# Order of the splits in an MLP's products, and its last two blocks run as one

## The chip, the cores and the metric

One core of one Trainium2 chip runs the whole kernel. The metric is the device time of one execution in microseconds (us), as the median of several.

## The reference

A trunk of two layers over T = 1040 tokens (16 meta tokens and 1024 of the sequence), model width 1024, all in float32. Each layer has a mixer and an MLP of 4096 hidden features with squared ReLU; a final norm follows.

```python
def rmsnorm(x, w):
    return x * lax.rsqrt(jnp.mean(x * x, -1, keepdims=True) + EPS) * w
def sq_relu_mlp(h, w_up, w_down):
    return jnp.square(jax.nn.relu(h @ w_up)) @ w_down
for layer in range(2):
    hn = rmsnorm(h, norm_mix[layer])
    h = h + (even_mixer(hn, ...) if layer == 0 else ssd_mixer(hn, ...))
    h = h + sq_relu_mlp(rmsnorm(h, norm_mlp[layer]), mlp_w_up[layer], mlp_w_down[layer])
h = rmsnorm(h, norm_final)[:, 16:]
```

## The kernel before

**Precision.** TensorE (PE) multiplies in a shortened float format (`fp32r`). So each factor is split into a rounded part `hi` and the rest `lo`, and each product is three matmuls: hi by hi, hi by lo and lo by hi (`mm3`, L176 to L181). A split is a cast on ScalarE (ACT) and, behind it, a subtraction `x - hi`. In `split2` (L379) these are L385 and L386; the subtraction runs on GpSimd (POOL) for a weight and on VectorE (DVE) for a token factor. `load_w` (L159) does the same for a whole row of 1024 weights that has come by DMA: cast L173, subtraction L174, on DVE in the MLP.

**Tokens.** The residual `h` stays in SBUF, features on the partitions, tokens on the free axis. Token tiles are i = 0, 1, 2 of 400, 384 and 256 tokens (384, 384 and 256 where the meta tokens are left out: layer 1's MLP).

**The MLP** (`mlp`, L389). The 4096 hidden features are 32 rows of 128, taken as 16 blocks of two (f = 0, 1). `up_unit` (L357) computes one token tile of one row: 24 matmuls into a PSUM tile `mm`, then the rectifier times the token's norm factor (DVE, L372) and the square (ACT, L373) into the hidden tiles `sq`. A block has six such units. Each block's share of the down projection is then added to `h`. The two rows of a block and the two halves of the tokens (520 each in layer 0, 512 in layer 1) form 2 x 2 quarters of the hidden values (`b11` to `b22`), and the weights have four quarters likewise (`w11` to `w22`).

- Blocks 0 to 13 take `seven` products (keys 1, 2, 5, 6, 3, 4, 7) of combined quarters in place of eight. POOL forms the combinations in `ca` (weights) and `cb` (tokens); both go through `split2`, into a ring of six buffers `pc`. A product (`product`, L486) is 48 matmuls of 260 columns in layer 0 and 24 of 512 in layer 1; its results are evicted from the PSUM tile `pd` by DVE's addition (L502) into `h` or into one of three running sums `acc1`, `acc6`, `acc7`. In block 0 those sums are written by ACT's copy (L500).
- Block 14 takes the `eight` plain products, two at a time, so four double products (c11, c21, c22, c12). Between them stand the six up units of block 15, and `combine` (L504, additions L505), which joins the three sums to `h`.
- Block 15 is the last part (L562 to L594). Its hidden values are split (L569 on ACT, L570 on DVE) into the room of `acc1` and `acc6`; then, for each token tile, each of the 8 output tiles n takes 6 matmuls and is evicted by L583 on DVE. Behind each eviction stand the next norm's squares (L587) and, in layer 1, the scaling by the final norm's weight (L591).

The next norm goes on from there: `token_sums` (L243) sums over the features on PE (L250), `rsqrt` (L184 to L196) takes the reciprocal root on DVE in three Newton steps, `token_bcast` (L263) spreads it on PE (L267), and `apply` (L287) scales, casts and splits the token tile for mixer 1 (L293, L295, L297). In layer 1 `final` (L321) multiplies by the spread root (L337 on DVE, L335 on POOL) and stores.

PSUM has eight banks. In the MLP's wide stage `pd` has three tiles of two banks, and `ps` (the `mm` tiles) two of one; else `ps` has four. In `mlp` the pieces of a product are split two products ahead of its matmuls:

```python
        sw = lambda x: self.split2(mp, x, pool)
        sx = lambda x: self.split2(mp, x, v)
            yield "1", [(sw(w11), sx(b11))]
```

The order on each engine is that of a list scheduler, which places the instructions when the kernel is built, by the program's order and its estimate of when each can start. Each engine then works in that order, and semaphores keep the dependences.

## Time and profile before

| | |
|---|---|
| median of 3 runs | 2789.8 us (2785.27 to 2791.72) |
| the profiled execution | 2793.77 us, its span 2792.0 us |
| instructions | 44635 |
| PE busy | 2677.5 us (96%), 17121 matmuls |
| PE's weight loads | 2554.3 us (91%) |
| DVE busy | 2118.9 us (76%), 3901 instructions |
| ACT busy | 1104.8 us (40%), 2275 |
| POOL busy | 1077.8 us (39%), 1005 |
| granted clock of PE, mean | 0.982 |

All times are of one profiled execution, from the span's start. Layer 0's MLP takes its first product at about 417 us; its last part runs from 1081.6 to 1110.5 us, and mixer 1 begins there. Layer 1's last part ends at 2773.2 us, and the last norm and the stores fill the rest. A busy share is a mean over stages with different limits. In a timeline's rows, `A<-B` is the tile written and the tiles read, `x2` says that two such instructions in a row are told as one, and brackets hold the idle time just before an instruction and what ended it.

### The profile page before, as it was taken

To read this page: it belongs to the slowest core of one execution; us is meant where nothing else is said; L and a number is where in the kernel's file an instruction comes from. 1 tells how busy PE (TensorE), PEld (TensorE's weight loads), DVE (VectorE), ACT (ScalarE), POOL (GpSimd) and SP (SyncE) were. 2 spreads that over 40 slices of the span, in tenths; PEclk is the share of its full clock that TensorE was granted. 3 is DMA by queue.
4 is the path that set the end of the run, shared out by engine and by line. 5 is a ranking of instruction groups with operands and counts; after the bars stand their busy time and mean duration, and the time that the engine had idled before them with its cause. 6 is when DMAs were issued, how large, how long until landed. Compare 5 with 4: busy or idle time off the path is not lost.

```text
span 2792.0 us, 44635 instructions
## 1 busy us (share of the span) xinstructions
PE 2677.5 (96%) x17121; PEld 2554.3 (91%) x17121; DVE 2118.9 (76%) x3901; ACT 1104.8 (40%) x2275; POOL 1077.8 (39%) x1005
## 2 busy tenths in 40 slices
PE   7998999999999999999999999999989999999997
PEld 7887999999999998899999999999978999999996
DVE  9887466777777787977767767677797777777786
ACT  4555353223322223453434434344454333333333
POOL 3212115445454432242333333334444455455432
PEclk9999999999999999999999999999999999999998
DMA  4432411111111110121212212123312111111101
GB/s 163 114 79 58 140 43 54 43 50 50 46 54 43 54 31 29 45 85 54 72 57 63 75 56 70 58 63 95 102 60 68 53 54 46 54 57 45 51 31 65
DMA packets 117909, 176.35 MB, mean 63 GB/s; under 512 B 13376, under 2 KB 47936, under 8 KB 117568
## 3 DMA queue, kind: packets, MB, share of 16 engines
q1 hardware_dynamic: 117408, 173.34, 20.0%
q8 instruction: 135, 2.21, 0.3%
q14 instruction: 78, 0.64, 0.1%
q10 hardware_dynamic: 288, 0.15, 0.0%
HBM read 158.34 MB, written 8.72 MB: 60 GB/s over the span
## 4 chain that ended last, share of the span: by engine, by line
PE 72%; DVE 19%; ACT 3%; issue 3%; POOL 2%; DMA 2%; SPq 0%; DVEq 0%; ACTq 0%; POOLq 0%
PE mm L179 16%; PE mm L180 16%; PE mm L181 16%; PE pd L179 6%; PE pd L181 6%; PE pd L180 6%; DVE xbc L1261 3%; DVE wlo L174 2%; DVE acc L502 2%; PE mm L1371 1%; ACT whi L173 1%; PE sm L1375 1%; DVE pc L386 1%; PE mm L1368 1%; PE sm L267 1%
## 5 line engine op out<-in xcount | busy, mean ns | idle before, releaser
L179 PE MATMUL mm<-hi,whi 128*128 128x384 f32 (+2 forms) x3120 | 1020.3, 327 | 19.7 <-ACT whi L173 9.8
L180 PE MATMUL mm<-lo,whi 128*128 128x384 f32 (+2 forms) x3120 | 1007.9, 323 | 0.8 <-DVE lo L940 0.4
L181 PE MATMUL mm<-hi,wlo 128*128 128x384 f32 (+2 forms) x3120 | 1005.7, 322 | 2.7 <-POOL wlo L174 2.7
L179 PEld LDWEIGHTS mm<-hi,whi 128*128 128x128 f32 x3120 | 593.8, 190 | 30.6 <-ACT whi L173 11.1
L180 PEld LDWEIGHTS mm<-lo,whi 128*128 128x128 f32 x3120 | 593.0, 190 | 8.8 <-POOL lo L297 2.0
L181 PEld LDWEIGHTS mm<-hi,wlo 128*128 128x128 f32 x3120 | 595.1, 191 | 3.8 <-POOL wlo L174 3.5
L179 PE MATMUL pd<-pc 128*128 128x260 f32 (+1 forms) x1272 | 408.0, 321 | 14.4 <-DVE acc L502 12.0
L180 PE MATMUL pd<-pc 128*128 128x260 f32 (+1 forms) x1272 | 404.2, 318 | 0.0
L181 PE MATMUL pd<-pc 128*128 128x260 f32 (+1 forms) x1272 | 404.1, 318 | 0.0
L502 DVE TENSOR_TENSOR h<-h,pd 128x520 f32<-128x520 f32 (+1 forms) x360 | 312.7, 871 | 68.0 <-PE pd L181 53.4
L386 POOL TENSOR_TENSOR pc<-draw,pc 128x512 fp32r<-128x512 f32 x96 | 131.7, 1375 | 419.9 <-ACT pc L385 409.6
L179 PEld LDWEIGHTS pd<-pc 128*128 128x128 f32 x1272 | 238.8, 188 | 34.9 <-DVE acc L502 18.7
L373 ACT ACTIVATE sq<-s 128x384 f32<-128x384 f32 (+2 forms) x192 | 94.3, 491 | 409.7 <-DVE s L372 409.6
L181 PEld LDWEIGHTS pd<-pc 128*128 128x128 f32 x1272 | 239.3, 188 | 16.6
L180 PEld LDWEIGHTS pd<-pc 128*128 128x128 f32 x1272 | 239.2, 188 | 13.1
L386 POOL TENSOR_TENSOR pc<-ca,pc 128x512 fp32r<-128x512 f32 x112 | 156.0, 1393 | 235.2 <-ACT pc L385 231.9
L173 ACT CAST whi<-wraw 128x512 fp32r<-128x512 f32 x286 | 167.2, 618 | 155.6 <-PE mm L180 137.6
L372 DVE SCALAR_TENSOR_TENSOR s<-mm,rb 128x384 f32<-128x384 f32 (+2 forms) x192 | 98.8, 515 | 170.4 <-PE mm L181 156.3
L1261 DVE SCALAR_TENSOR_TENSOR xbc<-s,cols,xbc 128x400 f32<-128x400 f32 (+2 forms) x288 | 202.7, 704 | 24.1 <-ACT xbc L1259 21.5
L502 DVE TENSOR_TENSOR acc<-acc,pd 128x520 f32<-128x520 f32 (+1 forms) x234 | 189.1, 859 | 4.0 <-PE pd L181 4.0
L174 DVE TENSOR_TENSOR wlo<-wraw,whi 128x512 fp32r<-128x512 f32 x224 | 167.0, 764 | 17.1 <-ACT whi L173 10.3
L386 DVE TENSOR_TENSOR pc<-cb,pc 128x520 fp32r<-128x520 f32 (+1 forms) x112 | 149.3, 1333 | 38.7 <-ACT pc L385 38.7
(381 smaller groups left out, 4424.6 us busy)
## 6 DMA issues: line engine op xcount, KB each, us to landing
wraw<-in_mlp_up SPq DMA_DIRECT2D x128, 256.0 KB
draw<-in_mlp_down SPq DMA_DIRECT2D x120, 256.0 KB
wraw<-in_ssd_in SPq DMA_DIRECT2D x120, 256.0 KB
csb<-csd SPq DMA_DIRECT2D x64, 256.0 KB
sa<-ecd SPq DMA_DIRECT2D x128, 64.0 KB
wraw<-in_ssd_out SPq DMA_DIRECT2D x32, 256.0 KB
wraw<-in_ev_in SPq DMA_DIRECT2D x24, 256.0 KB
wraw<-in_ev_out SPq DMA_DIRECT2D x18, 256.0 KB
```

The source lines that it names most:

```text
L173: nc.scalar.copy(hi[:, s], raw)
L174: e.tensor_tensor(out=lo[:, s], in0=raw, in1=hi[:, s].bitcast(F32), op=ALU.subtract)
L179: nc.tensor.matmul(pt, lhsT=whi, rhs=xhi, start=first, stop=False)
L180: nc.tensor.matmul(pt, lhsT=whi, rhs=xlo, start=False, stop=False)
L181: nc.tensor.matmul(pt, lhsT=wlo, rhs=xhi, start=False, stop=last)
L267: self.nc.tensor.matmul(st[:, o:o + l], lhsT=y[:l, i:i + 1].broadcast_to([l, P]), rhs=self.ident[:l, :l], start=True, stop=True)
L372: nc.vector.scalar_tensor_tensor(out=r, in0=pt[:, :w], scalar=0.0, in1=rbs[i], op0=ALU.max, op1=ALU.mult)
L373: nc.scalar.activation(out=dst[:, o - t0:o - t0 + w].bitcast(F32), in_=r, func=AF.Square)
L386: e.tensor_tensor(out=lo, in0=x, in1=hi.bitcast(F32), op=ALU.subtract)
L502: v.tensor_tensor(out=d, in0=d, in1=src, op=ALU.add)
L1261: v.scalar_tensor_tensor(out=ot, in0=raw[:, k:k + w], scalar=cw(k), in1=ot, op0=ALU.mult, op1=ALU.add)
L1368: nc.tensor.matmul(py[:, j * P:j * P + P], lhsT=H[:, 2 * j:2 * j + 2].rearrange("p r q -> p (r q)"), rhs=r["C"], start=True, stop=True)
```

## The change

- `pair` splits the token factor of a product first and then the weight factor; all seven products of a block use it. Before, the weight came first.
- `eight` is gone. Block 14 takes no products of its own any more. Its two rows and the two of block 15 are the four rows f = 0 to 3 of one plain product: in the last part each output tile takes 12 matmuls, not 6. For the first token tile the rows of block 14 of output tiles 0 to 3 come ahead of those of block 15.
- The three sums are joined to `h` during the six up units of block 15, with no products between. Block 14's hidden values are split in the same place, on ACT and POOL (L548, L549), into the room of `acc1` and `acc6`. Those of block 15 are split on ACT and DVE into the room of `acc7` and one more pair of `sq` tiles.
- The four weight rows are loaded as whole rows: two during the last two products of block 13, one at the fourth up unit, one behind the sixth (into the buffers `draw`). Their raw quarters are not loaded for block 14.
- In `psum`, the pool `ps` is taken before `pd`.

```diff
@@ -121,8 +121,8 @@
         self.pstack = st = ExitStack()
         self.npsum += 1
         pool = lambda name, bufs: st.enter_context(self.tc.tile_pool(name=f"{name}{self.npsum}", bufs=bufs, space=PSUM))
+        self.ps = pool("ps", 2 if wide else 4)
         self.pd = pool("pd", 3) if wide else None
-        self.ps = pool("ps", 2 if wide else 4)
         self.pss = None if wide else pool("pss", 4)
 
     def load_h(self, i, k0=0, k1=KT):
@@ -161,6 +161,8 @@
         pool = pool or self.wp
         if tag == "pc":
             hi, lo = (self.piece(pool)[:, :1024] for _ in range(2))
+        elif tag == "draw":
+            hi, lo = ([pool.tile([P, 512], F32R, name=tag, bufs=6) for _ in range(2)] for _ in range(2))
         else:
             bufs = 2 if tag == "o" else None
             hi = pool.tile([P, 1024], F32R, name=f"{tag}hi", bufs=bufs)
@@ -170,8 +172,9 @@
             s = slice(q * 512, q * 512 + 512)
             raw = self.wp.tile([P, 512], F32, name="wraw", bufs=3)
             nc.sync.dma_start(raw, ap[:, s])
-            nc.scalar.copy(hi[:, s], raw)
-            e.tensor_tensor(out=lo[:, s], in0=raw, in1=hi[:, s].bitcast(F32), op=ALU.subtract)
+            h, l = (hi[q], lo[q]) if tag == "draw" else (hi[:, s], lo[:, s])
+            nc.scalar.copy(h, raw)
+            e.tensor_tensor(out=l, in0=raw, in1=h.bitcast(F32), op=ALU.subtract)
         return hi, lo
 
     def mm3(self, pt, whi, wlo, xhi, xlo, first, last):
@@ -436,8 +439,9 @@
             (b11, b12), (b21, b22) = ((q[:, :hw].bitcast(F32), q[:, hw:].bitcast(F32)) for q in sq[b])
             return raws.pop(b), (b11, b12, b21, b22)
 
-        sw = lambda x: self.split2(mp, x, pool)
-        sx = lambda x: self.split2(mp, x, v)
+        def pair(w, x):
+            x = self.split2(mp, x, v)
+            return [(self.split2(mp, w, pool), x)]
 
         def seven(b):
 
@@ -450,37 +454,23 @@
                 if x0 is not None:
                     pool.tensor_tensor(out=cb, in0=x0, in1=x1, op=ALU.subtract)
 
-            yield "1", [(sw(w11), sx(b11))]
-            yield "2", [(sw(w12), sx(b21))]
+            yield "1", pair(w11, b11)
+            yield "2", pair(w12, b21)
             comb(w21, w22, ALU.add, b12, b11)
-            yield "5", [(sw(ca), sx(cb))]
+            yield "5", pair(ca, cb)
             comb(ca, w11, ALU.subtract, b22, cb)
-            yield "6", [(sw(ca), sx(cb))]
+            yield "6", pair(ca, cb)
             comb(w12, ca, ALU.subtract, None, None)
-            yield "3", [(sw(ca), sx(b22))]
+            yield "3", pair(ca, b22)
 
             pool.tensor_tensor(out=cb, in0=b21, in1=cb, op=ALU.subtract)
-            yield "4", [(sw(w22), sx(cb))]
+            yield "4", pair(w22, cb)
             comb(w11, w21, ALU.subtract, b22, b12)
-            yield "7", [(sw(ca), sx(cb))]
-
-        def eight(b):
-
-            (w11, w12, w21, w22), (b11, b12, b21, b22) = quarters(b)
-            a = sw(w11), sw(w12)
-            x = sx(b11), sx(b21)
-            yield "c11", list(zip(a, x))
-            a = sw(w21), sw(w22)
-            yield "c21", list(zip(a, x))
-            x = sx(b12), sx(b22)
-            yield "c22", list(zip(a, x))
-            a = sw(w11), sw(w12)
-            yield "c12", list(zip(a, x))
+            yield "7", pair(ca, cb)
 
         acc = {k: mp.tile([P, 4, hw], F32, name=f"acc{k}", bufs=1) for k in "167"}
         H = lambda r, c: self.H[:, 4 * r:4 * r + 4, halves[c]]
-        dest = {"1": acc["1"], "6": acc["6"], "7": acc["7"], "2": H(0, 0), "5": H(1, 1), "3": H(0, 1), "4": H(1, 0),
-                "c11": H(0, 0), "c12": H(0, 1), "c21": H(1, 0), "c22": H(1, 1)}
+        dest = {"1": acc["1"], "6": acc["6"], "7": acc["7"], "2": H(0, 0), "5": H(1, 1), "3": H(0, 1), "4": H(1, 0)}
         step = 2 if len(subs) == 1 else 1
 
         def product(key, pairs, copy):
@@ -520,66 +510,92 @@
         for n in range(0, 4, 2):
             d = H(0, 1)[:, n:n + 2]
             v.tensor_tensor(out=d, in0=d, in1=H(1, 1)[:, n:n + 2], op=ALU.subtract)
-        items = (it for b in range(NB - 1) for it in (seven(b) if b < NB - 2 else eight(b)))
+        items = (it for b in range(NB - 2) for it in seven(b))
         queue = deque()
-        fetch = lambda: queue.append(next(items))
+
+        def fetch():
+            it = next(items, None)
+            if it:
+                queue.append(it)
+
         fetch()
         fetch()
+        wd = []
         for b in range(NB - 2):
             u = ups(b + 1)
+            end = b == NB - 3
             for j in range(7):
-                if j == 3:
+                if j == 3 and not end:
                     rows(b + 1)
-                last = b == NB - 3 and j > 4
-                if not last:
-                    fetch()
-                elif j == 6:
-                    fetch()
+                fetch()
                 product(*queue.popleft(), b == 0)
+                if end and j > 4:
+                    wd.append(self.load_w(down[2 * NB - 9 + j], mp, "pc"))
                 next(u, None)
             for _ in u:
                 pass
+
         u = ups(NB - 1)
         com = combine()
-        for j in range(4):
-            if j < 3:
-                fetch()
-            else:
-                wd = [self.load_w(down[2 * NB - 2], mp, "pc")]
-            product(*queue.popleft(), False)
-            for _ in range(2):
-                next(u, None)
+        hid = []
+
+        def room(k):
+            t = mp.tile([P, 4, hw], F32R, name=f"acc{k}", bufs=1)
+            return [t[:, n:n + 2].rearrange("p a b -> p (a b)") for n in (0, 2)]
+
+        def parts(hl, q, c, e):
+            h, l = (z[:, c] for z in hl)
+            nc.scalar.copy(h, q[:, c].bitcast(F32))
+            e.tensor_tensor(out=l, in0=q[:, c].bitcast(F32), in1=h.bitcast(F32), op=ALU.subtract)
+
+        for j in range(6):
+            if j in (2, 4):
+                hid.append(room("16"[j // 2 - 1]))
+                for c in (slice(0, hw), slice(hw, 2 * hw)):
+                    parts(hid[-1], sq[NB - 2][j // 2 - 1], c, pool)
+            next(u, None)
+            if j == 3:
+                wd.append(self.load_w(down[2 * NB - 2], mp, "pc"))
+            next(com, None)
+            if j == 0 or j == 2:
                 next(com, None)
         for _ in u:
             pass
         for _ in com:
             pass
-        wd.append(self.load_w(down[2 * NB - 1], mp, "pc"))
+        wd.append(self.load_w(down[2 * NB - 1], mp, "draw"))
+        hid.append(room("7"))
+        hid.append(hidden(NB))
         self.psum(False)
         if nxt == "nmix1":
             self.ahead_bc()
-
-        hid = []
-        for k in "16":
-            t = mp.tile([P, 4, hw], F32R, name=f"acc{k}", bufs=1)
-            hid.append([t[:, n:n + 2].rearrange("p a b -> p (a b)") for n in (0, 2)])
         for o, w in tls:
-            c = slice(o - t0, o - t0 + w)
-            for (h, l), q in zip(hid, sq[NB - 1]):
-                nc.scalar.copy(h[:, c], q[:, c].bitcast(F32))
-                v.tensor_tensor(out=l[:, c], in0=q[:, c].bitcast(F32), in1=h[:, c].bitcast(F32), op=ALU.subtract)
+            for f in range(2):
+                parts(hid[2 + f], sq[NB - 1][f], slice(o - t0, o - t0 + w), v)
+
+        def last(pt, i, n, f):
+            o, w = tls[i]
+            (ah, al), (xh, xl) = wd[f], (z[:, o - t0:o - t0 + w] for z in hid[f])
+            if f == 3:
+                ah, al = ah[n // 4], al[n // 4]
+            ns = slice(n % 4 * P, n % 4 * P + P) if f == 3 else slice(n * P, n * P + P)
+            self.mm3(pt[:, :w], ah[:, ns], al[:, ns], xh, xl, f == 0, f == 3)
+
         end = nxt == "nfin"
         for i, (o, w) in enumerate(tls):
             off = o - TT[i][0]
             hs = lambda n: self.h[i][:, n, off:off + w]
-            pts = {}
             for n in range(KT):
-                for f, m in ((f, m) for f in range(2) for m in (range(n, n + 4) if n % 4 == 0 else ())):
-                    if f == 0:
-                        pts[m] = self.mm()
-                    ms = slice(m * P, (m + 1) * P)
-                    h, q = (z[:, o - t0:o - t0 + w] for z in hid[f])
-                    self.mm3(pts[m][:, :w], wd[f][0][:, ms], wd[f][1][:, ms], h, q, f == 0, f == 1)
+                if n == 0:
+                    pts = {m: self.mm() for m in range(4 if i == 0 else 1)}
+                    for fs in (0, 1), (2, 3):
+                        for m in pts:
+                            for f in fs:
+                                last(pts[m], i, m, f)
+                elif i or n > 3:
+                    pts = {n: self.mm()}
+                    for f in range(4):
+                        last(pts[n], i, n, f)
                 v.tensor_tensor(out=hs(n), in0=hs(n), in1=pts[n][:, :w], op=ALU.add)
                 self.tick()
                 if nxt is None:
```

**The orders.** Lines are numbered by each kernel's own text: the changed kernel's L176 and L177 are L173 and L174 of before, L388 and L389 are L385 and L386, L375 and L376 are L372 and L373, L492 is L502, L495 is L505, L599 is L583, L296 is L293.

*First order:* ACT in layer 0's steady part, the casts of a product's two factors (`ca` and `cb` combined ones, `sq` a plain token quarter; weights are 512 wide, tokens 520). Before:

```order
L385 CAST pc<-ca 128x512
L385 CAST pc<-cb 128x520
L373 ACTIVATE sq_8872<-s_8899 128x400
L385 CAST pc<-ca 128x512
L385 CAST pc<-sq_8399 128x520
L373 ACTIVATE sq_8872<-s_8967 128x384
```

Of the change:

```order
L388 CAST pc<-cb 128x520
L388 CAST pc<-ca 128x512
L376 ACTIVATE sq_8872<-s_8899 128x400
L388 CAST pc<-sq_8399 128x520
L388 CAST pc<-ca 128x512
L376 ACTIVATE sq_8872<-s_8967 128x384
```

In each pair the token's cast now stands ahead of the weight's; nothing else has moved.

*Second order:* DVE at the end of layer 0's MLP, from product 7 of block 13 on (its four evictions into `acc`, here `acc_3842`). Before:

```order
L502 TENSOR_TENSOR acc_3842<-acc_3842,pd 128x520 x4
L174 TENSOR_TENSOR wlo<-wraw,whi 128x512
L502 TENSOR_TENSOR h<-h,pd 128x520
L505 TENSOR_TENSOR acc_3842<-acc_3842,acc_3841 128x1040
L502 TENSOR_TENSOR h<-h,pd 128x520
L505 TENSOR_TENSOR acc_3842<-acc_3842,acc_3841 128x1040
L502 TENSOR_TENSOR h<-h,pd 128x520 x2
L505 TENSOR_TENSOR h<-h,acc_3840 128x2x520 x2
L386 TENSOR_TENSOR pc<-sq_10294,pc 128x520
L386 TENSOR_TENSOR pc<-sq_10295,pc 128x520
L372 SCALAR_TENSOR_TENSOR s_10815<-mm,rb_3898 128x400
L570 TENSOR_TENSOR acc_11200<-sq_10788,acc_11200 128x400
```

Of the change:

```order
L492 TENSOR_TENSOR acc_3842<-acc_3842,pd 128x520 x4
L177 TENSOR_TENSOR wlo<-wraw,whi 128x512 x2
L495 TENSOR_TENSOR acc_3842<-acc_3842,acc_3841 128x1040 x2
L375 SCALAR_TENSOR_TENSOR s_10753<-mm,rb_3898 128x400
L177 TENSOR_TENSOR pc<-wraw,pc 128x512 x2
L495 TENSOR_TENSOR h<-h,acc_3842 128x2x520 x2
L375 SCALAR_TENSOR_TENSOR s_10785<-mm,rb_3947 128x384
L495 TENSOR_TENSOR h<-h,acc_3842 128x2x520 x2
L375 SCALAR_TENSOR_TENSOR s_10820<-mm,rb_3979 128x256
L177 TENSOR_TENSOR draw<-wraw,draw 128x512
L177 TENSOR_TENSOR wlo<-wraw,whi 128x512
L549 TENSOR_TENSOR acc_10942<-sq_10726,acc_10942 128x400
```

Before, evictions of block 14's products into `h`, additions of `combine` and token splits alternate. Now the additions follow one another between the rectifiers of the up units and the splits of the weight rows.

*Third order:* DVE at the end of layer 0's last part: evictions of the third token tile (128x256), and the scaling of the first tile (128x400) for the mixer. Five of the eight evictions stand ahead of these rows in the kernel before. Before:

```order
L293 SCALAR_TENSOR_TENSOR s_11359<-h,cols,sm 128x400
L293 SCALAR_TENSOR_TENSOR s_11363<-h,cols,sm 128x400
L305 SCALAR_TENSOR_TENSOR lo_81<-h,cols,hi_78 128x256
L297 TENSOR_TENSOR lo_79<-s_11359,hi_76 128x400
L190 TENSOR_SCALAR rsy<-ts_s 128x3
L305 SCALAR_TENSOR_TENSOR lo_81<-h,cols,hi_78 128x256
L293 SCALAR_TENSOR_TENSOR s_11367<-h,cols,sm 128x400
L293 SCALAR_TENSOR_TENSOR s_11371<-h,cols,sm 128x400
L191 TENSOR_SCALAR rsy<-rsy 128x3
L297 TENSOR_TENSOR lo_79<-s_11367,hi_76 128x400
L193 SCALAR_TENSOR_TENSOR rst<-rsy 128x3
L583 TENSOR_TENSOR h<-h,mm 128x256
```

Of the change, where none of the eight stands ahead of these rows:

```order
L296 SCALAR_TENSOR_TENSOR s_11176<-h,cols,sm 128x400
L296 SCALAR_TENSOR_TENSOR s_11180<-h,cols,sm 128x400
L300 TENSOR_TENSOR lo_79<-s_11176,hi_76 128x400
L599 TENSOR_TENSOR h<-h,mm 128x384
L296 SCALAR_TENSOR_TENSOR s_11184<-h,cols,sm 128x400
L296 SCALAR_TENSOR_TENSOR s_11188<-h,cols,sm 128x400
L283 TENSOR_TENSOR sa<-sa,s_11309 128x384
L300 TENSOR_TENSOR lo_79<-s_11184,hi_76 128x400
L599 TENSOR_TENSOR h<-h,mm 128x256
L296 SCALAR_TENSOR_TENSOR s_11192<-h,cols,sm 128x400
L296 SCALAR_TENSOR_TENSOR s_11196<-h,cols,sm 128x400
L287 TENSOR_TENSOR sa<-sa 128x384
```

The first tile's eight scalings (L293, now L296) stood behind five of the third tile's evictions and among the rest; now four stand ahead of the first of these evictions, and the last two, a few rows further on, still ahead of the second.

## Rows read from the trace of the kernel before

**Rows 1.** Windows: stretch and length, busy us by engine, granted clock, DMA share, GB/s.

```profile
440.00:1000.00 560.00, 548.21 (x3946) 541.74 (x3945) 434.99 (x567) 168.13 (x306) 273.18 (x190) 1.00 0.15 47
2130.00:2690.00 560.00, 560.00 (x3071) 516.14 (x3070) 419.94 (x416) 180.03 (x326) 275.10 (x200) 1.00 0.16 51
1009.60:1031.90 22.30, 20.79 (x147) 20.18 (x145) 21.93 (x26) 5.97 (x11) 6.98 (x4) 1.00 0.08 24
1031.90:1081.60 49.70, 48.84 (x362) 48.64 (x361) 35.47 (x50) 14.24 (x28) 7.54 (x4) 1.00 0.11 33
1081.60:1110.50 28.90, 26.93 (x166) 25.50 (x166) 22.17 (x54) 14.05 (x31) 8.37 (x10) 1.00 0.10 33
1110.50:1140.00 29.50, 27.15 (x131) 23.42 (x132) 27.32 (x65) 14.75 (x32) 11.91 (x17) 0.88 0.04 10
2741.90:2773.00 31.10, 26.90 (x163) 26.14 (x162) 22.83 (x57) 19.48 (x43) 10.58 (x10) 0.95 0.14 52
```

**Rows 2.** Waits of PE, 440 to 1000 us: total us, times, longest us.

```profile
PE pd L179 <- DVE acc L502: 11.8, 24, 0.7
```

**Rows 3.** Timeline, 722.4 to 726.5 us: start, us, engine, line, operation.

```profile
722.56 0.62 ACT L385 CAST pc<-ca 128x512 fp32r<-128x512 f32 x1 [1.62 <-PE pd L181]
...
723.09 0.62 ACT L385 CAST pc<-cb 128x520 fp32r<-128x520 f32 x1
723.17 0.68 DVE L174 TENSOR_TENSOR wlo<-wraw,whi 128x512 fp32r<-128x512 f32 x1
723.26 1.76 POOL L386 TENSOR_TENSOR pc<-ca,pc 128x512 fp32r<-128x512 f32 x1 [4.45 <-ACT pc L385]
723.77 1.81 DVE L386 TENSOR_TENSOR pc<-cb,pc 128x520 fp32r<-128x520 f32 x1
...
725.50 1.29 DVE L502 TENSOR_TENSOR acc<-acc,pd 128x520 f32<-128x520 f32 x2
...
726.24 0.39 PE L179 MATMUL pd<-pc 128*128 128x260 f32 x1 [0.71 <-DVE acc L502]
```

**Rows 4.** Timelines of POOL and DVE, 710 to 712.5, 1030 to 1032 us.

```profile
710.39 1.29 POOL L386 TENSOR_TENSOR pc<-draw,pc 128x512 fp32r<-128x512 f32 x1 [2.44 <-ACT pc L385]
...
710.87 1.37 DVE L386 TENSOR_TENSOR pc<-sq,pc 128x520 fp32r<-128x520 f32 x1 [0.53 <-ACT pc L385]
...
1030.54 1.31 DVE L386 TENSOR_TENSOR pc<-sq,pc 128x520 fp32r<-128x520 f32 x2
```

**Rows 5.** Timeline of PE, 422 to 424 us: layer 0's MLP, first product.

```profile
423.33 0.39 PE L179 MATMUL pd<-pc 128*128 128x260 f32 x1 [1.08 <-DVE h L502]
```

**Rows 6.** Timeline of PE: first matmuls of both last parts and of mixer 1.

```profile
1081.62 0.42 PE L179 MATMUL mm<-acc,pc 128*128 128x400 f32 x1 [0.88 <-ACT pc L173]
...
1110.56 0.45 PE L179 MATMUL mm<-hi,whi 128*128 128x400 f32 x1 [0.92 <-ACT hi L295]
...
2744.05 0.41 PE L179 MATMUL mm<-acc,pc 128*128 128x384 f32 x1 [2.04 <-DVE h L502]
```

**Rows 7.** Timelines of PE and of DVE, 2772 to 2784 us.

```profile
2772.95 0.28 PE L181 MATMUL mm<-acc,pc 128*128 128x256 f32 x1
2775.51 1.65 PE L267 MATMUL sm<-ident,rsy 128*128 128x128 f32 x6 [2.28 <-DVE rsy L195]
...
2778.70 0.16 DVE L255 TENSOR_SCALAR ts_s<-sm 128x2 f32<-128x2 f32 x1 [2.85 <-PE sm L250]
2778.89 0.83 DVE L190 TENSOR_SCALAR rsy<-ts_s 128x2 int32<-128x2 int32 x1
2779.76 0.92 DVE L191 TENSOR_SCALAR rsy<-rsy 128x2 int32<-128x2 int32 x1
2780.59 1.93 DVE L337 TENSOR_TENSOR h<-h,sm 128x384 f32<-128x384 f32 x4
```

**Rows 8.** Timelines of POOL and of DVE, 16.5 to 17.5 us.

```profile
15.18 2.94 POOL L174 TENSOR_TENSOR wlo<-wraw,whi 128x512 fp32r<-128x512 f32 x2 [3.13 <-ACT whi L173]
...
16.85 1.71 DVE L280 TENSOR_TENSOR sa<-sa,s 128x400 f32<-128x400 f32 x1
```

## The prediction

> **What bounds the kernel now.** I read the table of busy time by stretch first. In both MLPs TensorE (PE) is the bound: 548.21 of 560 us in the steady part of layer 0's MLP, all 560 in layer 1's [rows 1]. So a step is worth only the PE time that it frees: idle time, or time at the lower of PE's two clocks. I counted that stretch by stretch. Layer 0, steady: 11.8 us idle. Layer 0's end: 22.30 - 20.79 = 1.5, then 49.70 - 48.84 = 0.9, then 28.90 - 26.93 = 2.0 us. The stretch behind it, where the mixer begins: 2.35 us idle at a granted clock of 0.88. Layer 1's end: 4.2 us idle at 0.95 [rows 1].
>
> Then the waits of PE in the steady part: 24 of them, 11.8 us, the longest 0.7, all for the same releaser, VectorE's (DVE's) eviction of a product [rows 2]. Then the order of time around one such wait, with all engines [rows 3]: PE stands 0.71 us until 726.24 because a PSUM buffer comes free only with the first eviction of 725.50, and that stands in DVE's queue behind the token remainder `pc<-cb` of 723.77, which took 1.81 us.
>
> Why 1.81? Alone the same subtraction takes 1.31 / 2 = 0.65 us; next to a GpSimd (POOL) weight remainder it takes 1.37, ending 0.56 us after POOL's end [rows 4]. 710.39 + 1.29 = 711.68, and 710.87 + 1.37 = 712.24: DVE stood until POOL was done. In rows 3 the same holds: POOL ends at 725.02, DVE at 725.58. And the other way: POOL's 1.76 us are its usual 1.29 behind the end of DVE's `wlo` at 723.85 [rows 3, 4]. These two kinds of work exclude each other; whoever is first holds the other up.
>
> **The change, part by part.**
>
> *A, token first.* ScalarE (ACT) casts in pairs. Before, the weight cast (722.56) released POOL at 723.26, and the token cast followed 0.53 us later [rows 3]. Now the pair is turned (first order shown), so POOL's request moves by 0.53 us to 723.79, while DVE's stays at 723.77: it is bound there by its own `wlo`, not by ACT. DVE's order is unchanged. If DVE is first, the remainder takes 0.65 in place of 1.81 us, the eviction comes 1.1 us earlier, and the wait of 0.71 us is covered. The 24 waits are of two kinds: 12 like this one, and 12 of (11.8 - 12 x 0.71) / 12 = 0.27 us, in which DVE's `wlo` stands behind a POOL combination that the change moves by under 0.1 us; I leave these. So 12 x 0.71 = **8.5 us** go. At other pairs DVE gains as much but nothing waits for it; in layer 1 PE never stands [rows 1], so 0 there. POOL's remainders come 0.5 to 1.2 us later; their users are products two further on, over 5 us away, so that costs nothing; if that cover failed, it would cost at most the delay, 1.2 us a block.
>
> The first block pays. Its weight halves were split ahead, behind other work; now two of them queue behind the tokens. The four ACT copies that free the first PSUM buffers follow the casts, and PE's first product starts earlier than its buffers turn round. I put a wait of some 2 us in place of the one of 1.08 at 423.33 [rows 5]: +1.0. Bounds 0 and +2. A together: **-7.5**.
>
> *B, end of layer 0.* Block 14's four double products with 16 evictions (0.65 us each, the pace of the row of 725.50 [rows 3]: 10 us of DVE) and ten splits go. Its 192 matmuls of 260 columns become 144 of 400, 384 and 256: the same 49,920 columns. PE now runs product 7 of block 13, then six up units of block 15, then one long part. DVE, 35.47 of 49.70 us busy there [rows 1], does the additions of the three sums meanwhile (second order shown); POOL splits block 14. Of the 1.5 us idle I keep 0.8 (DVE still adds up early, in front of evictions): -0.7. The 0.88 us before the last part, for the last rows' cast [rows 6], go, since these rows are loaded during the up units and used third and fourth: -0.9. In the last part each output tile now takes 12 matmuls, not 6, so DVE and ACT have twice the time for it; but DVE also does the next norm there, so I keep its 1.1 us. B: **-1.6**, between 0 and -3.2.
>
> *C, start of the mixer.* Idle 0.92 us before 1110.56 [rows 6], 2.35 us after it, and (1 - 0.88) x 29.5 = 3.5 us at the half clock that followed the waits: 6.8 us [rows 1]. All of it is PE waiting for the normed first token tile, as DVE came to it only at the end of the last part. With the long last part (some 11 us for the last token tile where there were 6) DVE's scaling stands ahead of seven of the eight last evictions (third order shown), so the first tile is ready when PE arrives. The second tile's scaling comes after the last eviction and still loses some 2 us. C: **-4.8**, between 0 and -6.8.
>
> *D, end of layer 1.* Idle 4.2 us (of it the wait of 2.04 until the eviction that precedes the last part [rows 6]), and (1 - 0.95) x 31.1 = 1.6 us of half clock: 5.8. The last evictions of block 14 are gone, and the first half of the last part needs no result of the up units just done. I keep 0.8 for narrower matmuls (384 and 256 columns for 512). D: **-5.0**, between 0 and -5.8.
>
> *E, tail.* Behind PE's last product matmul (2772.95) the chain runs through the last tile's sums, three Newton steps and the output. In its way stand work of the middle tile: its broadcast on PE (2775.51), ahead of the sums; the reciprocal root's first two steps, 0.83 and 0.92 for 0.16 us, next to POOL's multiplications; and four multiplications of 1.93 us [rows 7]. With the last tile's matmuls lasting twice as long the middle tile is done before. 1.1 + 0.67 + 0.76 + 1.9, and 0.6 for evictions that lagged: **-5.0**, between 0 and -6.
>
> **Sum.** -7.5 - 1.6 - 4.8 - 5.0 - 5.0 = -23.9 us against the profiled execution's 2793.8, so 2769.9. The median of the runs shown is 4.0 below that execution: **2766 us**.
>
> **The rule to weigh.** DVE's request leads POOL's by 0.02 us in A. In one place POOL was running when DVE started (two remainders fill 15.18 to 18.12), and DVE took 1.71 us, until 18.56; in another DVE began 0.09 us before POOL (723.17 against 723.26), and POOL was late [rows 3, 8]: so far the first has won, but no row has a lead as small as 0.02 us. The Trainium skill, "SBUF — State Buffer", section "Who interferes with whom", says that a DVE instruction with two SBUF inputs and a GpSimd instruction that reads SBUF exclude each other, and whoever issues first holds the pair of ports throughout. By that rule A is the -8.5 above. The same rule speaks against the new POOL splits of block 14: each may hold one of DVE's additions for its whole length.
>
> **Rivals.**
> 1. *POOL wins the tie.* The remainder at 723.77 then still takes 1.8 us and the 12 waits stay. For it: 0.02 us is less than the scatter of a semaphore. Against: rows 3 and 8. Time 2766 + 8.5 = **2774.5**. Chance 0.25.
> 2. *DVE is late anyway in the two last parts*, so C and E fall away: its load (27.32 of 29.5 us around the mixer's start [rows 1]) is what made these waits, and moving the scaling forward moves evictions back. Against: the part lasts 17 us longer on PE, and its work is the same. Time 2766 + 9.8 = **2776**. Chance 0.15.
> 3. *Slower: DVE becomes the bound in the six up units.* Between product 7 and the first use of block 15's halves it has four evictions, the rest of the additions, six rectified units, four row splits and the halves themselves. I reckon it ready some 6 us before PE needs them; four POOL splits of 1.29 us may each hold it up. Every microsecond past that margin costs 1 us per layer, and the half clock after it another 1.6 to 3.5 [rows 1]. It decides from some 10 us late per layer on; then 2 x (10 + 3) eats the whole gain, about **2792**. Chance 0.04.
>
> A case of no change, through several of these at once, has 0.06; my forecast keeps 0.5. That the change would not do what it says is excluded by the orders shown.
>
> **How the numbers follow.** A difference of 0.2%, 5.6 us, is about what a measurement here can tell from none. Faster beyond it: 0.5 + 0.25 + 0.15 = 0.90; within it 0.06; slower 0.04. The range: with every wait counted gone, 11.8 + 3.2 + 6.8 + 5.8 + 6 = 33.6 below the median, 2756; upwards both rivals 1 and half of 2, 2766 + 8.5 + 5 = 2780.
>
> **What would show it.** A: in layer 0's steady part the waits for evictions fall from 24 to about 12, of 0.3 us, and the subtraction `pc<-cb` behind `wlo` takes about 0.7. C: no idle before the mixer's first matmul and a granted clock near 1 there. D: no wait ahead of layer 1's last part. E: some 14 us from the last product matmul to the end of the span, not 19. The forecast is wrong if waits of several microseconds stand inside the six up units or at the first use of the last rows, or if layer 1's steady part shows PE idle.

## The result and the profile after

| | before | after |
|---|---|---|
| median, four runs each | 2790.76 us | 2762.35 us |
| lowest to highest | 2785.27 to 2793.59 | 2759.71 to 2762.97 |
| profiled execution | 2793.77 us | 2759.71 us |

The ratio is 0.9899, its 95% interval 0.9882 to 0.9916: 28.4 us faster. The forecast was 23.8 (2789.8 to 2766), its range 2756 to 2780. The two profiled executions lie 34.1 us apart, since that of before is 3.0 above its median and that of after 2.6 below; what follows by stage adds up to that 34.

The table of busy time by stretch, cut at the same instructions of PE in both traces (columns as in [rows 1]): layer 0's steady part, the end of its MLP, the start of mixer 1, the rest of the mixer, layer 1's steady part, the end of its MLP, the tail. Before:

```profile
493.20:990.60 497.40, 486.58 (x3511) 480.63 (x3510) 389.87 (x508) 148.97 (x271) 240.21 (x167) 1.00 0.15 48
990.60:1109.40 118.80, 114.62 (x800) 112.25 (x798) 92.88 (x145) 38.05 (x74) 34.59 (x26) 1.00 0.11 33
1109.40:1142.20 32.80, 29.02 (x142) 24.39 (x140) 30.59 (x77) 16.82 (x35) 12.61 (x19) 0.90 0.03 9
1142.20:2115.30 973.10, 939.87 (x6222) 897.70 (x6222) 738.00 (x1748) 437.41 (x1009) 354.40 (x453) 0.98 0.23 70
2115.30:2612.40 497.10, 497.10 (x2726) 458.10 (x2725) 368.45 (x365) 162.39 (x294) 246.43 (x180) 1.00 0.16 52
2612.40:2773.00 160.60, 156.40 (x867) 144.77 (x866) 122.05 (x160) 57.65 (x113) 57.21 (x42) 0.99 0.12 38
2773.00:2792.00 19.00, 4.60 (x20) 4.01 (x19) 10.69 (x37) 3.81 (x11) 3.84 (x4) 0.57 0.39 138
```

After:

```profile
493.20:977.30 484.10, 481.61 (x3510) 479.35 (x3509) 331.59 (x508) 147.90 (x271) 225.97 (x167) 1.00 0.15 48
977.30:1093.60 116.30, 113.72 (x752) 112.10 (x751) 90.10 (x146) 40.57 (x81) 33.88 (x27) 1.00 0.12 38
1093.60:1119.90 26.30, 23.82 (x144) 22.32 (x143) 26.23 (x75) 13.54 (x29) 10.55 (x18) 1.00 0.04 12
1119.90:2090.50 970.60, 935.60 (x6218) 892.69 (x6217) 733.34 (x1733) 435.81 (x1007) 355.77 (x450) 0.99 0.23 71
2090.50:2588.30 497.80, 497.79 (x2728) 458.81 (x2729) 326.85 (x365) 161.90 (x295) 259.76 (x181) 1.00 0.16 51
2588.30:2745.20 156.90, 156.21 (x921) 148.31 (x919) 112.26 (x165) 60.80 (x117) 63.49 (x44) 1.00 0.14 47
2745.20:2757.80 12.60, 2.65 (x15) 2.06 (x13) 5.78 (x23) 1.80 (x4) 0.00 (x0) 0.59 0.33 115
```

| stretch | forecast | lengths | measured |
|---|---|---|---|
| A, steady part | -7.5, of it +1.0 for the first block | 497.4 to 484.1 | -13.3 |
| B, end of layer 0 | -1.6 | 118.8 to 116.3 | -2.5 |
| C, mixer's start | -4.8 | 32.8 to 26.3 | -6.5 |
| rest of the mixer | 0 | 973.1 to 970.6 | -2.5 |
| layer 1's steady part | 0 | 497.1 to 497.8 | +0.7 |
| D, end of layer 1 | -5.0 | 160.6 to 156.9 | -3.7 |
| E, tail | -5.0 | 19.0 to 12.6 | -6.4 |

Every term A to E has its sign and place. The first block lies ahead of these stretches: both traces stand at the same matmul at 493.2 us. One of the twelve long waits that A counts stands in B's stretch (0.70 us, at 992.59 in the kernel before). The rest of the mixer isn't a part of the change's work: in a second execution of the changed kernel that stretch was another 3.7 us shorter. The 0.7 us that layer 1 loses come with the order of the PSUM pools (e5).

**A.** PE's waits in the steady part (440 to 1000 us were 24, 11.8 us [rows 2]); after, from 440 us on:

```profile
PE pd L182 <- DVE acc L492: 2.9, 13, 0.2
```

The timeline at the place of [rows 3], after (columns as there):

```profile
716.48 0.63 ACT L388 CAST pc<-cb 128x520 fp32r<-128x520 f32 x1 [1.63 <-PE pd L184]
...
717.08 0.68 DVE L177 TENSOR_TENSOR wlo<-wraw,whi 128x512 fp32r<-128x512 f32 x1
...
717.68 0.69 DVE L389 TENSOR_TENSOR pc<-cb,pc 128x520 fp32r<-128x520 f32 x1
717.76 1.77 POOL L389 TENSOR_TENSOR pc<-ca,pc 128x512 fp32r<-128x512 f32 x1 [4.40 <-ACT pc L388]
...
718.29 1.29 DVE L492 TENSOR_TENSOR acc<-acc,pd 128x520 f32<-128x520 f32 x2
...
719.28 0.28 PE L182 MATMUL pd<-pc 128*128 128x260 f32 x1
```

DVE's token remainder takes 0.69 us where it took 1.81, and now POOL is the one held up (1.77). The eviction starts 0.61 us behind the remainder, and PE's product follows with no idle time. At all 25 such places of this trace the remainder takes 0.68 or 0.69 us, and DVE starts 0.07 to 0.10 us ahead of POOL; at the 24 places of the kernel before it took 1.78 to 1.81.

**C and E.** DVE, the first tile's scaling (L296) among the last evictions (L599), and the mixer's first matmul on PE:

```profile
1084.43 1.34 DVE L296 SCALAR_TENSOR_TENSOR s<-h,cols,sm 128x400 f32<-128x400 f32 x2
...
1087.84 1.16 DVE L296 SCALAR_TENSOR_TENSOR s<-h,cols,sm 128x400 f32<-128x400 f32 x2
...
1095.62 0.41 DVE L599 TENSOR_TENSOR h<-h,mm 128x256 f32<-128x256 f32 x1
```

```profile
1093.59 0.28 PE L184 MATMUL mm<-sq,draw 128*128 128x256 f32 x1
1093.70 0.34 PE L182 MATMUL mm<-hi,whi 128*128 128x400 f32 x1
```

The last two pairs of scalings run 9 and 6 us ahead of the last part's end, so the mixer's first matmul starts 0.11 us after the last product's, with no idle time (0.92 us before [rows 6]), and at the full clock, 1.00 against 0.90. In the tail the middle tile's four multiplications now run at 2740.11, ahead of the last evictions, and the root's first steps take 0.17 us each, where [rows 7] have 0.83 and 0.92:

```profile
2740.11 1.94 DVE L340 TENSOR_TENSOR h<-h,sm 128x384 f32<-128x384 f32 x4
...
2748.15 0.17 DVE L193 TENSOR_SCALAR rsy<-ts_s 128x2 int32<-128x2 int32 x1
2748.35 0.17 DVE L194 TENSOR_SCALAR rsy<-rsy 128x2 int32<-128x2 int32 x1
```

**D.** The wait of 2.04 us before layer 1's last part [rows 6] is one of 0.52, for the rectifier of the last up unit:

```profile
2696.67 0.45 PE L182 MATMUL mm<-acc,pc 128*128 128x384 f32 x1 [0.52 <-DVE s L375]
```

### The profile page after: what moved, and what is told of

Read it like the earlier page. It is cut to its first block, busy times and chain, and to the rows that moved or that the text cites. A ratio compares the mean times of both kernels' runs of the same rounds, so it can differ in the third digit from the quotient of the medians.

```text
span 2757.8 us, 44764 instructions
## 1 busy us (share of the span) xinstructions
PE 2659.5 (96%) x17121; PEld 2546.9 (92%) x17121; DVE 1983.9 (72%) x3877; ACT 1102.3 (40%) x2271; POOL 1075.3 (39%) x1001
## 4 chain that ended last, share of the span: by engine, by line
PE 74%; DVE 16%; issue 3%; ACT 3%; DMA 2%; POOL 1%; SPq 0%; DVEq 0%; ACTq 0%; POOLq 0%
PE mm L182 16%; PE mm L183 16%; PE mm L184 16%; PE pd L182 6%; PE pd L184 6%; PE pd L183 6%; DVE xbc L1277 3%; DMA csb<-csd 1%; DVE wlo L177 1%; PE mm L1387 1%; PE sm L1391 1%; PE mm L1384 1%; ACT whi L176 1%; DVE lo L308 1%; PE sm L1350 1%
## 5 line engine op out<-in xcount | busy, mean ns | idle before, releaser
L182 PE MATMUL pd<-pc 128*128 128x260 f32 (+1 forms) x1176 | 375.7, 319 | 7.4 <-DVE acc L492 2.9
L184 PE MATMUL pd<-pc 128*128 128x260 f32 (+1 forms) x1176 | 373.7, 318 | 0.0
L183 PE MATMUL pd<-pc 128*128 128x260 f32 (+1 forms) x1176 | 373.4, 318 | 0.0
L492 DVE TENSOR_TENSOR h<-h,pd 128x520 f32<-128x520 f32 (+1 forms) x336 | 291.9, 871 | 59.0 <-PE pd L184 44.7
L375 DVE SCALAR_TENSOR_TENSOR s<-mm,rb 128x384 f32<-128x384 f32 (+2 forms) x192 | 98.7, 515 | 259.9 <-PE mm L184 247.0
L389 POOL TENSOR_TENSOR pc<-ca,pc 128x512 fp32r<-128x512 f32 x112 | 171.0, 1527 | 240.1 <-ACT pc L388 160.5
L389 POOL TENSOR_TENSOR pc<-draw,pc 128x512 fp32r<-128x512 f32 x84 | 125.7, 1496 | 335.2 <-ACT pc L388 335.2
L182 PEld LDWEIGHTS pd<-pc 128*128 128x128 f32 x1176 | 221.0, 188 | 23.1 <-DVE acc L492 5.6
L184 PEld LDWEIGHTS pd<-pc 128*128 128x128 f32 x1176 | 221.2, 188 | 15.3
L183 PEld LDWEIGHTS pd<-pc 128*128 128x128 f32 x1176 | 221.0, 188 | 12.0
L376 ACT ACTIVATE sq<-s 128x384 f32<-128x384 f32 (+2 forms) x192 | 94.2, 491 | 343.8 <-DVE s L375 343.6
L176 ACT CAST whi<-wraw 128x512 fp32r<-128x512 f32 x286 | 167.8, 617 | 154.4 <-PE mm L183 136.4
L492 DVE TENSOR_TENSOR acc<-acc,pd 128x520 f32<-128x520 f32 (+1 forms) x234 | 190.3, 862 | 4.1 <-PE pd L184 4.0
L177 DVE TENSOR_TENSOR wlo<-wraw,whi 128x512 fp32r<-128x512 f32 x224 | 168.7, 772 | 17.3 <-ACT whi L176 9.1
L388 ACT CAST pc<-cb 128x520 fp32r<-128x520 f32 (+1 forms) x112 | 69.9, 625 | 248.9 <-PE pd L184 130.5
```

The costliest lines, as they stand in the source:

```text
L176: nc.scalar.copy(h, raw)
L177: e.tensor_tensor(out=l, in0=raw, in1=h.bitcast(F32), op=ALU.subtract)
L182: nc.tensor.matmul(pt, lhsT=whi, rhs=xhi, start=first, stop=False)
L183: nc.tensor.matmul(pt, lhsT=whi, rhs=xlo, start=False, stop=False)
L184: nc.tensor.matmul(pt, lhsT=wlo, rhs=xhi, start=False, stop=last)
L375: nc.vector.scalar_tensor_tensor(out=r, in0=pt[:, :w], scalar=0.0, in1=rbs[i], op0=ALU.max, op1=ALU.mult)
```

## The experiments

Ratios are to the kernel before, run beside each on the same chip, with 95% intervals. The changed kernel itself, run again beside e10:

> The changed kernel itself, beside the one above on the same chip: 0.989 to 0.9905 of the kernel before, 2761 to 2764.

Measured: 2761.61 us, 0.9896 (0.9879 to 0.9912).

**e1, the swap alone**

```diff
-            yield "1", [(sw(w11), sx(b11))]
+            yield "1", pair(w11, b11)
...
```

> The kernel before with the token factor split first in all seven products of a block, in both layers; the last two blocks as before. Theory (in layer 0 the token remainder of one product a block no longer stands behind a weight remainder on POOL, so the eviction behind it comes 1.1 us earlier): the twelve long waits of PE in layer 0's steady part go, 24 waits of 11.8 us become 12 to 13 of under 4 us; by the starts of matmuls in the two profiles that is worth 10 to 13 us, so a median of some 2779 against 2791; nothing changes in layer 1 or at the ends of the MLPs. Rival (the gain of the change lies in the joined blocks, and the steady part gained by something that comes with them): within 3 us of the kernel before, with the waits still there.

Measured: 2777.42 us against 2792.57, 0.9947 (0.9934 to 0.9959), 15.2 us faster, more than the 10 to 13 expected. The steady stretch takes 484.2 us, as in the changed kernel, and the end of layer 0 is 1.1 us shorter, about the worth of the twelfth long wait. From there to the last part's end in layer 1 the distance to the trace of before changes by no more than 3 us: the end of layer 1 takes 2.5 us longer, and the tail is 3.0 us shorter.

**e2, the joined blocks alone**

```diff
-            x = self.split2(mp, x, v)
-            return [(self.split2(mp, w, pool), x)]
+            w = self.split2(mp, w, pool)
+            return [(w, self.split2(mp, x, v))]
```

> The changed kernel with the weight factor split first again; only the joined last blocks and what goes with them remain of the change. Theory: layer 0's steady part keeps its 24 waits of some 12 us; the two ends, the start of the mixer and the tail gain what the trace of the change shows there, 15 to 21 us, so 2770 to 2776. Rival (the two halves of the change need each other, since the joined part starts from a product that is late when the token remainder is late): under 10 us of gain, over 2781.

Measured: 2778.69 us, 0.9953 (0.994 to 0.9967), 13.9 us faster. That is under the 15 to 21 expected by the profile and over the rival's 10. The steady stretch takes 497.4 us, as before, and every other stretch is as in the changed kernel to within 0.7 us. 15.2 + 13.9 = 29.1 is the whole change within the scatter: the two halves don't need each other.

**e3, one pair of casts in fourteen blocks**

```diff
-            yield "5", [(sw(ca), sx(cb))]
+            yield "5", [(sw(ca), sx(cb)) if layer else (sx(cb), sw(ca))[::-1]]
```

> The kernel before with the token factor split first in product 5 of layer 0 alone: 14 pairs of casts turned of 196. Theory: these are the pairs at which an eviction that PE waits for stands behind the token remainder, so this one turn brings all that turning every pair brings: the same twelve waits go, 2779 to 2782. Rival (every turned pair gives its share, through less of DVE's time lost): a fourteenth of it, under 1 us, and most of the waits stay.

Measured: 2780.23 us, 0.996 (0.9947 to 0.9972), 12.3 us faster. The steady stretch takes 486.6 us. (The text's "14 pairs of 196": 14 blocks, 7 pairs, two layers.)

**e4, the same remainder on POOL, no pair turned**

```diff
-            yield "5", [(sw(ca), sx(cb))]
+            yield "5", [(sw(ca), self.split2(mp, cb, pool) if layer == 0 else sx(cb))]
```

> The kernel before, weight first, but the token remainder of product 5 in layer 0 is computed by POOL behind the weight remainder, not by DVE. No pair of casts is turned. Theory (what costs is that DVE stands in its queue for POOL, ahead of an eviction): DVE goes straight on to the evictions, and the same twelve waits go, 2779 to 2784; POOL's other work comes 1.3 us later once a block, which costs nothing. Rival (it is the order of the casts, or when POOL's weight remainder is done): the waits stay or move, 2788 or more.

Measured: 2782.13 us, 0.9968 (0.9956 to 0.9979), 10.4 us faster. The steady stretch takes 488.7 us. The waits of PE, 493 to 973 us, in e1, e2, e3 and e4:

```profile
PE pd L179 <- DVE acc L506: 2.5, 11, 0.2
```

```profile
PE pd L182 <- DVE acc L492: 10.8, 22, 0.7
```

```profile
PE pd L179 <- DVE acc L502: 3.9, 11, 0.4
```

```profile
PE pd L179 <- DVE acc L502: 3.5, 11, 0.4
```

The long waits (0.7) are gone in e1, e3 and e4; e2 keeps them. e3 turns 14 pairs and gets 12.3 of e1's 15.2 us, in the steady stretch 10.9 of 13.2. e4 turns none, and its POOL is still held up by `wlo` at the same place (1.76 us), but DVE has no remainder there to stand on and goes on to the evictions:

```profile
718.49 0.68 DVE L174 TENSOR_TENSOR wlo<-wraw,whi 128x512 fp32r<-128x512 f32 x1
718.58 1.76 POOL L386 TENSOR_TENSOR pc<-ca,pc 128x512 fp32r<-128x512 f32 x1 [4.45 <-ACT pc L385]
...
719.09 1.90 DVE L502 TENSOR_TENSOR acc<-acc,pd 128x520 f32<-128x520 f32 x3
```

So it is neither the order of the casts as such nor POOL's time that counts, but what stands between DVE and the eviction.

**e9, the last part in two rounds**

```diff
+        for i, (o, w) in enumerate(tls):
+            for n in range(KT):
+                pt = self.mm()
+                for f in (0, 1):
+                    last(pt, i, n, f)
+                d = self.h[i][:, n, o - TT[i][0]:o - TT[i][0] + w]
+                v.tensor_tensor(out=d, in0=d, in1=pt[:, :w], op=ALU.add)
         for i, (o, w) in enumerate(tls):
...
+                    for f in (2, 3):
```

> The changed kernel, but the last part runs in two rounds: first block 14's two rows over all token tiles, with 24 evictions of their own, then block 15's two rows as in the kernel before (6 matmuls to an eviction). The PE work is the same. Theory (the mixer's start and the tail gained because the last token tile takes 11 us instead of 6, with 8 evictions, so DVE gets to the scaling of the first tile and to the middle tile's norm): these gains go again, 5 to 8 us at the mixer's start and 4 to 6 in the tail, so 10 to 14 us over the changed kernel, ratio to before 0.9935 to 0.995. Rival (what helped is that combine and the evictions of block 14's products no longer lie just ahead of the last part): the gains stay, within 4 us of the changed kernel, ratio 0.99 to 0.9915.

Measured: 2776.84 us, 0.9944 (0.9929 to 0.996), slower than the changed kernel by 14.5 us (medians) or 13 (ratios, 0.0045 to 0.0048 of 2793). The mixer's start and the tail of this kernel (columns as in [rows 1], cut as in the tables of the result) are those of the kernel before: 32.6 us at a clock of 0.90, where that one has 32.8 and the changed kernel 26.3, and a tail of 18.7.

```profile
1096.50:1129.10 32.60, 28.92 (x142) 24.29 (x140) 30.59 (x77) 16.59 (x34) 12.73 (x20) 0.90 0.03 9
...
2756.60:2775.30 18.70, 4.58 (x20) 4.00 (x19) 10.71 (x37) 3.83 (x11) 3.85 (x4) 0.56 0.40 141
```

In its tail DVE's rows read as in [rows 7]:

```profile
2762.51 0.83 DVE L193 TENSOR_SCALAR rsy<-ts_s 128x2 int32<-128x2 int32 x1
2763.37 0.92 DVE L194 TENSOR_SCALAR rsy<-rsy 128x2 int32<-128x2 int32 x1
2764.20 1.93 DVE L340 TENSOR_TENSOR h<-h,sm 128x384 f32<-128x384 f32 x4
```

So C and E come from the last part's one long accumulation, not from moving `combine` and block 14's evictions away. The two rounds shorten the last token tile and double the evictions at once; which of these counts, no run separates.

**e6, block 14 split on DVE**

```diff
-                    parts(hid[-1], sq[NB - 2][j // 2 - 1], c, pool)
+                    parts(hid[-1], sq[NB - 2][j // 2 - 1], c, v)
```

> The changed kernel with block 14's hidden values split by DVE, not POOL. Theory (POOL's splits hold DVE's additions, but DVE has spare time in the six up units, so neither costs PE anything): within 2 us of the changed kernel, ratio to before 0.9893 to 0.9907. Rival 1 (four remainders more on DVE make it late at the end of the MLP): 3 to 10 us slower than the changed kernel. Rival 2 (POOL's holding of DVE is what leaves PE's short waits there): 1 to 3 us faster.

Measured: 2761.47 us, 0.9888 (0.9871 to 0.9904): as the changed kernel. In the changed kernel POOL's splits do hold DVE's additions (two beside them took 4.62 us, the two that followed 2.38), and the rectifier of an up unit (1032.00) stands behind them. Little of it reaches PE: no listed wait there in this trace, one of 0.38 us in that of the second execution, none in e6's. In e6's trace the end of layer 0 is 1.3 us shorter than in the changed kernel's, and the mixer's start 1.5 us longer. DVE's timeline of the changed kernel:

```profile
1027.45 4.62 DVE L495 TENSOR_TENSOR h<-h,acc 128x1040 f32<-128x1040 f32 x2
1032.00 0.54 DVE L375 SCALAR_TENSOR_TENSOR s<-mm,rb 128x384 f32<-128x384 f32 x1
1032.47 2.38 DVE L495 TENSOR_TENSOR h<-h,acc 128x1040 f32<-128x1040 f32 x2
```

**e5, the old order of the PSUM pools** (`pd` taken ahead of `ps`)

> The changed kernel with the PSUM pools taken in the old order. Theory (the order decides only which banks the first product of an MLP inherits from the last up units, and so a wait of some 2 us at its start in layer 0, and none in layer 1): within 2.5 us of the changed kernel either way, with the wait ahead of the first product at another place. Rival (the order is needed for the gains, since the first products in the kernel before started on banks that were free earlier): 3 us or more slower or faster, with the steady part unchanged.

Measured: 2760.1 us, 0.9881 (0.9865 to 0.9898); the intervals overlap, so no difference is shown. The changed kernel's wait of 2.19 us before layer 0's first product, for the rectifier of an up unit, is gone; one of 1.1 us for an eviction stands again where [rows 5] have it. Two more things change in its trace: neither last part has the wait of 0.52 us for a rectifier, and layer 1's steady part takes 497.1 us, not 497.8. The other runs agree. The waits of 2.19 and the 497.8 us are in all kernels with the new order (e2, e6, e8, e9 too) and in none with the old one (before, e1, e3, e4, e10). By these stretches the new order costs some 2 to 3 us (an estimate from the traces), less than the times here can tell apart.

**e8, one more step: a weight remainder to POOL.** In the changed kernel a shorter wait is left once a block: `wlo` stands behind POOL's combination (1.15 us), and the eviction behind that. The timeline of the changed kernel:

```profile
736.16 1.33 POOL L455 TENSOR_TENSOR cb<-sq,sq 128x520 f32<-128x520 f32 x1
...
736.89 1.15 DVE L177 TENSOR_TENSOR wlo<-wraw,whi 128x512 fp32r<-128x512 f32 x1
...
738.70 0.39 PE L182 MATMUL pd<-pc 128*128 128x260 f32 x1 [0.24 <-DVE acc L492]
```

```diff
-                    W[n] = self.load_w(up[n])
+                    W[n] = self.load_w(up[n], lo_pool=layer == 0 and f == 0 and b > 0)
```

> The changed kernel, with the remainder of one of a block's two up rows (f = 0) computed by POOL, in layer 0, from block 1 on. Meant to remove the waits that are left in layer 0's steady part, twelve of 0.4 to 0.5 us, in which DVE's remainder of a weight row stands behind a combination on POOL and an eviction stands behind that. Theory: they go, 4 to 6 us faster than the changed kernel, ratio to before 0.9875 to 0.989. Rival (POOL's two remainders more a block, 2.6 us in 43, hold up DVE at other places, ahead of other evictions): no gain or a loss, 0.9895 to 0.993.

Measured: 2755.62 us, 0.9869 (0.9851 to 0.9887), a little better than expected. The steady stretch of this kernel takes 478.8 us, PE busy in all of it, 5.3 us less than in the changed kernel, where eleven waits of 2.5 us in all were listed (columns as in [rows 1]):

```profile
494.50:973.30 478.80, 478.80 (x3510) 478.79 (x3509) 317.15 (x486) 147.88 (x271) 248.62 (x189) 1.00 0.16 49
```

**e10, e8 with the old order of the pools**

> The changed kernel with block remainders of one up row on POOL in layer 0 and the PSUM pools in the old order, both at once. Theory (the two act at different places, 6 us in the steady part and 1 to 2 at the first products): the sum, ratio to before 0.985 to 0.987, 6 to 9 us faster than the changed kernel run beside it. Rival (POOL's longer work in the first blocks delays the first products more when they start earlier): no better than the former alone, 0.987 to 0.988.

Measured: 2754.56 us, 0.9864 (0.9849 to 0.9878), 7 us faster than the changed kernel beside it and the fastest of all; against e8 no difference is shown.

## Why the prediction was right, and where its terms were off

- **A, mechanism right, size too small.** The turn gives DVE the lead, the remainder takes 0.69, the twelve long waits go and twelve short ones stay; layer 1 gains nothing. Rival 1 (POOL wins the tie) didn't come true, but its tie wasn't run either: the lead is 0.07 to 0.10 us, not 0.02, since POOL now starts 0.13 us behind the end of its cast, where it was 0.08 before. DVE's start was put right. The term mis-sized is "12 x 0.71". The idle time of a wait isn't what it costs. In the trace of before the matmul ahead of the one at 726.24 started at 725.18, 1.06 us earlier, where such matmuls stand 0.18 apart, and the one after followed 0.22 behind it, where 0.12 is usual: 0.88 + 0.10, so near 0.98 for a wait listed as 0.71. Summed over all matmuls of the stretch, which holds eleven of the long waits, lost time fell from 17.1 to 5.5 us: 11.6 in place of 11 x 0.71 = 7.8. e8 shows the same: waits listed as 2.5 us were worth 5.3. The other 1.7 us are matmuls that stand closer by half a nanosecond on average, in e1 too; no run shows why.
- **A, the first block.** "I put a wait of some 2 us in place of the one of 1.08": there is one of 2.19, but its cause was argued wrong. It is not the weight halves that queue behind the tokens: e1 has that order and loses nothing there, and e2 has the wait without that order. It comes with the order of the PSUM pools (e5), which the prediction gave no cost. From the last broadcast before the products to the matmul near 493.3 us the trace takes 81.4 us before, 81.8 after and 81.2 in e1 and e5: about 0.5 lost, not 1.0.
- **B** gained 2.5 for 1.6, but some 1.0 of it is A's twelfth long wait (1.1 in e1). The 1.5 left fit the term by luck, as its parts don't. For the products ahead of the up units 0.8 us of waits was kept; there are 1.9 (0.78, 0.22 and 0.89; the first is new and in neither e1 nor e2). The wait of 0.88 before the last part, counted as gone, is one of 0.52 for the last rectifier, and it comes with the pools (e5). In the last part 1.1 was kept; 0.16 is left.
- **C, mechanism shown by e9, size too small** (6.5 for 4.8). By the starts of matmuls this stretch lost 10.0 us before and 3.6 after. I had 6.8 from idle time and clock, the same misreading as in A; that the second tile still waits was right (2.5 us idle).
- **D** gained 3.7 for 5.0. The idle time fell from 4.2 to 0.7, not to 0: the rectifier's 0.52 is new and comes with the pools. With the old order (e5) the stretch is 0.7 us shorter still. PE's busy time fell by 0.2 where 1.6 of half clock less 0.8 for narrower matmuls was put. The 0.8 was right (96 of 512 columns, 0.227 apart, became 96 of 384, 0.176 apart, and 48 of 256, 0.116 apart: 0.7 more); the missing 0.6 isn't traced.
- **E, shown by e9** (6.4 for 5.0). The end came 12.6 us behind the last product, not 14; the root's two steps gained 1.4 (0.67 + 0.76 put), and the other parts of the sum weren't measured one by one.
- **Rivals 2 and 3.** DVE wasn't late in the last parts (one wait of 0.16 or 0.15 us for it in each), and the six up units had room: with the additions held up PE waits 0.4 us there at most (second execution; e6).
- **The rule on the ports.** The Trainium skill, "SBUF — State Buffer", section "Who interferes with whom", lets whoever issues first hold the pair. The trace agrees at leads of 0.07 to 0.10 us (717.68 against 717.76 above); no run has a smaller one. The rule's warning against block 14's splits on POOL holds for DVE (4.62 us) and costs PE 0.4 us at most.

One sentence on the kernel before was wrong: a product is 24 matmuls in layer 0 and 12 in layer 1, not 48 and 24; no term used it. And POOL's end in [rows 3] is 1.17 us behind that of `wlo` (725.02 against 723.85), not its usual 1.29; the order of who holds whom stays.

## What to carry to other kernels

Where the work of two engines holds each other up, as DVE's and POOL's does here, look for the one place where the loser stands ahead of work that the bounding engine waits for: turning that one pair, or moving that one instruction to the other engine, brought four fifths (e3) or two thirds (e4) of what turning all brought. Price a wait of TensorE by the starts of its matmuls, not by the listed idle time: here the listed 7.8 us were worth 11.6 and the listed 2.5 were worth 5.3. Try a change that only rides along, here the order of two pools, by itself: this one cost some 2 to 3 us by the traces and brought nothing that they show. And where the next stage's first work must get into an engine's queue, a longer accumulation with fewer evictions in the stage before makes the room.

## What the runs showed that was not expected

Which DVE instructions POOL holds up: two evictions, with one input in PSUM, took 1.29 us beside POOL's remainder (718.29 above) and as long without it (725.50 in [rows 3]), and the four multiplications with a PSUM factor took 1.93 us beside POOL's multiplications in the kernel before and 1.94 after. But the root's steps on 128 x 2 integers, with a single input, took 0.83 and 0.92 us beside POOL's multiplications and 0.17 without; the prediction had noted that as a fact, and e9 brought it back.
